# Spreading the roots' columns in a two-layer hybrid decoder trunk: transpositions on TensorE in place of fp32 products with the identity

## The chip, the core and the metric

The kernel runs on one core of a Trainium2 chip. Its time is the device time of one execution in microseconds (us); the median of several executions is given, with the lowest and the highest. Beside it stands one execution that was recorded by the hardware profiler: its span, its rows and its waits come from that execution alone.

## What is computed

The reference is a stack of two pre-norm residual layers over 1024 tokens of 1024 channels, in fp32, with a last RMSNorm. Each norm is followed by a shift and a scale from a conditioning vector. Cut to what matters here:

```python
def rms_norm(x, g):
    y = x * lax.rsqrt(jnp.mean(x * x, axis=-1, keepdims=True) + EPS)
    return y * g

for i in range(2):
    h = modulate(rms_norm(x, norm_mix_g[i]), sh_m, sc_m)
    y = conformer_conv(h) if i == 0 else multiscale_pool(h)   # the first has a LayerNorm inside
    x = x + (1.0 + g_m) * y
    h = modulate(rms_norm(x, norm_ffn_g[i]), sh_f, sc_f)
    x = x + (1.0 + g_f) * swiglu_ffn(h)
return rms_norm(x, final_g)
```

So each token has one reciprocal root per norm: two RMSNorms in each layer, the LayerNorm of the convolution module, and the last norm.

## The kernel before

Channels lie on the partitions and tokens along the free axis, in 8 tiles of 128 channels. The tokens are worked on in two chunks of 512, A and B, which are staggered: while one chunk is in its products, the other is in its norms. The large products are done in fp32r with three products for each tile of weights (high by high, high by low, low by high; `products`, line 496), so that TensorE has the longest queue. Part of the feed-forward products is done by a scheme with seven in place of eight products per block.

A norm needs a sum over channels, that is over partitions, for each token, and then the root of it along the free axis again, the same in every partition. `mean_rsqrt` (line 531) does it in these steps, and it is the one function that the change touches:

1. TensorE multiplies the squares, already summed over the 8 tiles, by a column of ones (lines 540 to 542). The sums of 512 tokens then stand as 4 columns of 128 partitions (the tile `var`).
2. VectorE works the reciprocal root out on those 128x4 values by eight or nine small instructions (`rsqrt`, line 504), into the tile `col`.
3. TensorE spreads each column along the free axis (line 558): the column, broadcast to 128x128, is the stationary operand and the identity the moving one, so that each of 128 output partitions receives the 128 roots in a row. The four results fill one PSUM bank (the tile `rstd`).
4. The norm multiplies the channels by it, from PSUM directly or from a copy by ScalarE (the tile `ny`).

`mean_rsqrt` is entered for twelve spreads: at the first norm of chunk A (line 1709), for that of chunk B, for the two LayerNorms (line 896), for the norms ahead of the feed-forward parts (lines 646 and 1284), for the pool layer's norms (line 956), for the last norm of A (line 1653), and for the two halves of the last norm of B (line 1577), which have two columns each; all others have four. The spread of column `i` is written as

```python
matmul(r[:, i * P : (i + 1) * P], col[:, i : i + 1].broadcast_to([P, P]), ident, start=True, stop=True)
```

The order of TensorE's instructions is the order in which the program emits them. That order is worked out while the program is built, by a planner with a clock for each engine: each product adds its price to `clock["PE"]` (line 147: 128 columns in fp32 cost `128 / 2400 * 4 + 0.0025` us), each instruction of VectorE and GpSimd adds a price to its own clock. After each unit of products, `pace` (line 224) emits waiting tasks of VectorE and GpSimd (norms, convolution taps, halves of weights) as long as the clock of their engine is less than 4 us ahead of TensorE's; `either` (line 179) gives an instruction to VectorE or GpSimd, whichever is free first by those clocks; and a task that has just asked for a root is not taken up again before `clock["PE"]` has moved on by the amount in `DELAY` (3.4 us for the spread, line 70). The instructions of the other engines are ordered by a scheduler from these.

Of the kernel before, what the change touches and what calls it, by code (L numbers as in the profile page):

```python
# [16 lines left out]
P = 128  # L17
# [114 lines left out]
def trunk(ctx, tc, xT, c, vec, ada, adan, w1f, w1, wdg, w2, wgu, wdn, wds, wpl, out):  # L132
    nc = tc.nc
    ctx.enter_context(tc.manual_schedule(engines={mybir.EngineType.PE}))
    clock = {"PE": 0.0, "V": 0.0, "G": 0.0, "S": 0.0}
# [5 lines left out]
    last_mm = [None]  # L141
# [3 lines left out]
    def matmul(out, lhsT, rhs, start, stop, more=False):  # L145
        n = out.shape[-1]
        clock["PE"] += n / 2400 * (1 if rhs.dtype == F32R else 4) + 0.0025
        last_mm[0] = nc.tensor.matmul(out, lhsT, rhs, start=start, stop=stop, skip_group_check=more).ins.name  # L148

    def order(ins):  # L150

        if behind[0] and last_mm[0] is not None:
            tc.add_manual_dep(ins.ins, last_mm[0], edge, reason="behind the products")
        return ins
# [41 lines left out]
    def nm(s):  # L196
        uid[0] += 1
        return f"{s}_{uid[0]}"
# [98 lines left out]
    def bank(name):  # L297
        return ps.tile([P, 512], F32, tag="mm", name=nm(name))

    def spare_bank(name):  # L300

        return ps.tile([P, 512], F32, tag="ca", name=nm(name), bufs=2)
# [11 lines left out]
    def temp(n, name="t", bufs=0):  # L314
        t = tmp.tile([P, TMPW], F32, tag=name if bufs else "t", name=nm(name), bufs=bufs or 4)
        return t[:, :n]
# [39 lines left out]
    ident = cst.tile([P, P], F32, name="ident")  # L356
# [80 lines left out]
    def ada_columns(js):  # L437


        todo = [(j, k) for j in js for k in range(KT)]  # L440
        src = lambda j, k: adan[k, :, (j - 2) * D : (j - 1) * D]
        ws = [ada_load(src(*t)) for t in todo[:ADA_BUFS]]
        for i, (j, k) in enumerate(todo):
            yield "load"
            if k == 0:
                acc = bank("ada")
            w = ws.pop(0)
            for g in range(4):
                matmul(acc[32 * g : 32 * g + 32, :Q], ccols[:, k, :], w[:, g * Q : g * Q + Q], start=k == 0, stop=k == KT - 1)
            clock["PE"] -= 1.3  # L450
            if i + ADA_BUFS < len(todo):
                ws.append(ada_load(src(*todo[i + ADA_BUFS])))
            if k == KT - 1 and (j != 3 or not held[0]):
                yield from columns_done(j, acc)
            elif k == KT - 1:
                held_back.append((j, acc))
# [3 lines left out]
    def columns_done(j, acc):  # L460

        rows = temp(Q)
        S_.copy(rows, acc[:, :Q])
        yield "spread"
        cols = bank("adac")
        for h in range(2):
            matmul(cols[:, 4 * h : 4 * h + 4], rows[:, h * P : h * P + P], quarters, start=True, stop=True)
        m = mod[:, j * KT : (j + 1) * KT]
        V_.tensor_tensor(m.rearrange("p (q h) -> p q h", h=2), cols[:, :KT].rearrange("p (h q) -> p q h", h=2),
                         V("ada_b", j * KT, KT).rearrange("p (q h) -> p q h", h=2), op=ADD)  # L470
        ada_gains(0, j, 0, KT, G_)
        ada_done.add((0, j))
# [23 lines left out]
    def products(out, wt, k, act, first, last, o=0, n=None, more=False):  # L496

        wk = slice(k * P, (k + 1) * P)
        for i, (wp, a) in enumerate(((0, 0), (0, 1), (1, 0))):
            cols = act[a][:, o : o + n] if n else act[a]  # L500
            matmul(out, wt[:, wp, wk], cols, start=first and i == 0, stop=last and i == 2, more=more)


    def rsqrt(v, y, t, q, alone):

        V_.tensor_scalar(y.bitcast(I32), v.bitcast(I32), -0.5, float(0x5F3759DF), op0=MUL, op1=ADD)
        yield
        V_.tensor_tensor(t, v, y, op=MUL)
        yield
        if not alone:  # L510
            V_.tensor_tensor(t, t, y, op=MUL)
            yield
            V_.tensor_scalar(q, t, 1.0, -10.0 / 3.0, op0=MUL, op1=ADD)
            yield
            V_.tensor_tensor(t, t, q, op=MUL)
            yield
        else:
            V_.tensor_tensor(q, t, y, op=MUL)
            yield
            V_.scalar_tensor_tensor(t, q, -10.0 / 3.0, q, op0=ADD, op1=MUL)  # L520
            yield
        V_.scalar_tensor_tensor(y, t, 5.0, y, op0=ADD, op1=MUL)
        yield
        V_.tensor_tensor(t, v, y, op=MUL)
        yield
        V_.scalar_tensor_tensor(t, t, -0.5 * 0.375**3, y, op0=MUL, op1=MUL)
        yield
        V_.scalar_tensor_tensor(y, t, 1.5 * 0.375, y, op0=ADD, op1=MUL)
        yield

    def mean_rsqrt(acc, n, keep=False, when="stats", loose=False, early=False):

        count = n // P
        parts = acc if isinstance(acc, list) else [acc]
        yield when
        b = bank("var")
        for i in range(count):  # L540
            for a in parts:
                matmul(b[:, i : i + 1], a[:, i * P : (i + 1) * P], ones[:, 0:1], start=a is parts[0], stop=a is parts[-1])
        v, t = b[:, :count], b[:, 16 : 16 + count]
        cols = tmp.tile([P, 16], F32, tag="col1", name=nm("col"), bufs=1)
        col, q = cols[:, :count], cols[:, 8 : 8 + count]
        for _ in rsqrt(v, col, t, q, "T" not in st or "taps_done" in st):
            if loose:
                yield
        V_.spent += 0.2
        clock["V"] += 0.2  # L550
        done = V_.last.ins.name
        for ins in [] if loose else recent + (beside if early else []) + [lows[id(wt)][0] for wt in st.get("loaded", [])[1:] if id(wt) in lows]:
            tc.add_manual_dep(ins, done, edge, reason="behind the root")
        recent.clear()
        yield "spread" if loose else "root"
        r = spare_bank("rstd") if "taps_done" in st else bank("rstd")
        for i in range(count):
            matmul(r[:, i * P : (i + 1) * P], col[:, i : i + 1].broadcast_to([P, P]), ident, start=True, stop=True)
        r = r[:, :n]
        if not keep:  # L560
            return r
        held = temp(n, "ny", 2)
        S_.copy(held, r)
        return held
# [54 lines left out]
    def rms(ch, keep=False):  # L619
        acc = yield from sum_sq(x[ch.i], ch.n)  # L620
        return (yield from mean_rsqrt(acc, ch.n, keep))
# [19 lines left out]
    def norm(ch, l, ffn, key, keep=False, squares=None):  # L641
        blocks = [block(f"h{ch.i}", "h") for _ in range(KT)]
        h = st[key] = [(b[:, 0], b[:, 1]) for b in blocks]
        st["blocks", ch.i] = blocks
        if squares is not None:
            rstd = yield from mean_rsqrt(squares.acc, ch.n, keep, loose=ch.i and not l)
        else:
            rstd = yield from rms(ch, keep)
        quiet[0] = ffn and not l
        for k in range(KT):  # L650
            if k == HOLD_TAPS:
                quiet[0] = False
            modulated(ch, l, ffn, h, rstd, k)
            yield
# [205 lines left out]
    def layer_norm_silu(ch):  # L860
# [30 lines left out]
        if ch.i == 0:  # L891
            for ins in beside:
                tc.add_manual_dep(ins, V_.last.ins.name, edge, reason="behind the sums")
            recent.extend(beside[2:])
            beside.clear()
        rstd = yield from mean_rsqrt(acc, n, when="settled" if ch.i else "stats", early=not ch.i)
        S_.activation(tmp.tile([P, 16], F32, tag="col0", name=nm("col"), bufs=1)[:, 0:1], acc[:, 0:1], AF.Silu)
        hv = [pair(f"h{ch.i}", "v") for _ in range(KT)]
# [1135 lines left out]
```

## Time and profile before

| | us |
|---|---|
| median of 3 executions | 1707.15 |
| lowest and highest | 1706.41 and 1709.43 |
| the profiled execution, its own time | 1708.65 |
| its span in the profile | 1706.9 |
| DVE busy | 1318.9 |
| ACT busy | 799.5 |
| POOL busy | 483.1 |

PE is TensorE's products, PEld its loads of stationary operands, DVE VectorE, ACT ScalarE, POOL GpSimd. "Busy" is the share of the span in which an engine ran an instruction; the products' ends are modelled, so a busy PE is not a PE at its peak. In the timeline's rows the columns are the start, the length, the engine, the line, the operation with output and inputs and shapes, and the count of instructions merged in the row; in brackets stands how long the engine was idle ahead of it, and what released it. In the chain's rows the columns are the start, the length, and the engine with the tile it wrote. The line is that of a helper in most rows (148 for products, 126 for the other engines), so that rows are told apart by their tiles.

The profiled execution took 1.75 us more than its span, which lies ahead of the first and behind the last recorded instruction, and 1.5 us more than the median of the three.

### The profile page before, as it was taken

The numbers are of one execution on the slowest core, as the hardware profiler recorded it, in microseconds if no ns is written. First come the engines' busy times: TensorE is split into PE (matmuls) and PEld (weight loads), VectorE is DVE, ScalarE is ACT, GpSimd is POOL, SyncE is SP. The second block draws the span as 40 slices with busy tenths as digits, with TensorE's granted clock in tenths as the row PEclk, the third lists the DMA queues.
The fourth block names the chain that finished last, engine by engine and source line by source line (L and its number), as shares of the span: only waits on it lengthen the run. The fifth ranks groups of instructions, "written<-read, shape, count | busy, mean of one in ns | idle before, by whom it ended". The sixth has DMA issues, their size and how long they took to land.

```text
span 1706.9 us, 21328 instructions
## 1 busy us (share of the span) xinstructions
PE 1671.0 (98%) x7614; PEld 1361.9 (80%) x7614; DVE 1318.9 (77%) x1872; ACT 799.5 (47%) x1085; POOL 483.1 (28%) x566
## 2 busy tenths in 40 slices
PE   7999999999999999999999999999999999999996
PEld 5777777778887888888888888888888888887776
DVE  8889899899659887878665987858777767657575
ACT  3669686866546333333213446637222222334353
POOL 3587767796001111211110311101111111010103
PEclk9999999999999999999999999999999999999998
DMA  8858987827776788986877757866777777486822
GB/s 303 286 168 228 237 229 196 220 96 225 225 238 152 253 272 279 294 249 229 342 256 264 250 173 206 241 237 190 189 209 234 217 229 217 169 294 191 241 93 99
DMA packets 115821, 380.71 MB, mean 223 GB/s; under 512 B 12225, under 2 KB 14401, under 8 KB 115714
## 3 DMA queue, kind: packets, MB, share of 16 engines
q1 hardware_dynamic: 77888, 247.46, 41.0%
q0 software_dynamic: 36736, 130.83, 31.2%
q8 instruction: 60, 0.98, 0.2%
q10 hardware_dynamic: 1090, 1.05, 0.2%
q14 instruction: 47, 0.39, 0.1%
HBM read 311.92 MB, written 63.18 MB: 220 GB/s over the span
## 4 chain that ended last, share of the span: by engine, by line
PE 86%; DVE 6%; DMA 3%; ACT 1%; issue 1%; POOL 1%; SPq 0%; DVEq 0%; ACTq 0%
PE a L148 23%; PE dn L148 21%; PE e L148 13%; PE p L148 12%; PE y L148 6%; PE g L148 3%; PE first L148 3%; PE tap L148 2%; DMA raw<-in_wds_dram 2%; POOL pa L126 1%; PE ada L148 1%; DVE t L126 1%; DMA adaw<-in_adan_dram 1%; DMA op<-kinds 1%; DVE x L126 1%
## 5 line engine op out<-in xcount | busy, mean ns | idle before, releaser
L126 ACT CAST w<-raw 128x1024 fp32r<-128x1024 f32 (+1 forms) x249 | 258.9, 1041 | 365.2 <-PE dn L148 99.7
L148 PE MATMUL dn<-g,w 128*128 128x512 f32 x1152 | 265.2, 391 | 1.7 <-DVE g L126 1.0
L126 DVE TENSOR_TENSOR w<-raw,w 128x1024 fp32r<-128x1024 f32 x177 | 217.7, 1233 | 51.2 <-ACT w L126 50.9
L148 PEld LDWEIGHTS dn<-g,w 128*128 128x128 f32 x1152 | 215.7, 188 | 47.6 <-DVE g L126 1.3
L148 PE MATMUL a<-n,w 128*128 128x512 f32 x1056 | 247.7, 390 | 1.1 <-DVE n L126 0.7
L148 PE MATMUL p<-h,w 128*128 128x512 f32 x1056 | 244.2, 391 | 0.9 <-DVE h L126 0.7
L126 POOL TENSOR_TENSOR pa<-pa,pr 128x512 f32<-128x512 f32 x160 | 228.4, 1512 | 23.0 <-ACT pr L126 16.6
L148 PEld LDWEIGHTS a<-n,w 128*128 128x128 f32 x1056 | 197.9, 188 | 44.0 <-DVE n L126 2.2
L148 PEld LDWEIGHTS p<-h,w 128*128 128x128 f32 x1056 | 197.3, 188 | 43.8 <-DVE h L126 1.5
L148 PE MATMUL dn<-hi,w 128*128 128x512 f32 (+1 forms) x600 | 174.3, 373 | 4.3 <-DVE x L126 2.4
L126 DVE SCALAR_TENSOR_TENSOR ca<-u,vecs,ca 128x512 f32<-128x512 f32 x245 | 169.7, 745 | 0.5
L126 DVE SCALAR_TENSOR_TENSOR x<-dn,gains,x 128x512 f32<-128x512 f32 (+1 forms) x144 | 100.9, 730 | 44.7 <-PE dn L148 44.6
L148 PEld LDWEIGHTS dn<-hi,w 128*128 128x128 f32 x600 | 109.8, 188 | 25.6 <-DVE x L126 3.2
L148 PE MATMUL a<-t,w 128*128 128x512 f32 x528 | 123.6, 390 | 0.7 <-DVE w L126 0.7
L148 PE MATMUL e<-b,w 128*128 128x512 f32 x528 | 123.4, 390 | 0.6 <-DVE r L126 0.6
L148 PE MATMUL e<-t,w 128*128 128x512 f32 x528 | 123.3, 389 | 0.0
L126 ACT ACTIVATE pr<-u,vecs 128x512 f32<-128x512 f32 x160 | 108.2, 716 | 26.0 <-POOL pa L126 18.2
L148 PEld LDWEIGHTS a<-t,w 128*128 128x128 f32 x528 | 99.0, 188 | 21.6 <-DVE w L126 1.1
L148 PEld LDWEIGHTS e<-b,w 128*128 128x128 f32 x528 | 99.1, 188 | 21.5 <-DVE r L126 1.0
L1108 POOL DMA_DIRECT2D raw<-in_wgu_dram x41 | 36.2, 884 | 282.5 <-DVE r L126 78.3
L148 PEld LDWEIGHTS e<-t,w 128*128 128x128 f32 x528 | 99.1, 188 | 20.5
L148 PE MATMUL dn<-lo,w 128*128 128x512 f32 (+1 forms) x300 | 111.7, 372 | 0.0
(181 smaller groups left out, 2380.2 us busy)
## 6 DMA issues: line engine op xcount, KB each, us to landing
raw<-in_wgu_dram SPq DMA_DIRECT2D x132, 512.0 KB, 4.8
adaw<-in_ada_dram POOLq DMA_DIRECT2D x48, 512.0 KB, 7.3
raw<-in_wdn_dram SPq DMA_DIRECT2D x44, 512.0 KB, 8.1
raw<-in_wgu_dram POOLq DMA_DIRECT2D x41, 512.0 KB, 7.4
raw<-in_w_dram SPq DMA_DIRECT2D x36, 512.0 KB, 6.2
gd<-g POOLq DMA_DIRECT2D x36, 512.0 KB, 8.1
g<-gd SPq DMA_DIRECT2D x36, 512.0 KB, 6.0
kinds<-k POOLq DMA_DIRECT2D x33, 512.0 KB, 7.3
```

What stands on the lines that cost most here:

```text
L126: self.last = self.order(getattr(self.eng, name)(out, *args, **kw))
L148: last_mm[0] = nc.tensor.matmul(out, lhsT, rhs, start=start, stop=stop, skip_group_check=more).ins.name
L1108: d = order(nc.gpsimd.dma_start(w[i], wgu[l, fp, src], accum_op=ADD))
```

## The change

The spread calls a new helper, which issues a transposition on TensorE with the same two operands (the broadcast column and the identity) into the same place, and adds another price to the planner's clock: `128 / 2400 + 0.0025` us for each column in place of `128 / 2400 * 4 + 0.0025`.

```diff
+    def turned(out, columns):
+
+        clock["PE"] += P / 2400 + 0.0025
+        last_mm[0] = nc.tensor.transpose(out, columns, ident).ins.name
...
         r = spare_bank("rstd") if "taps_done" in st else bank("rstd")
         for i in range(count):
-            matmul(r[:, i * P : (i + 1) * P], col[:, i : i + 1].broadcast_to([P, P]), ident, start=True, stop=True)
+            turned(r[:, i * P : (i + 1) * P], col[:, i : i + 1].broadcast_to([P, P]))
         r = r[:, :n]
```

Number and shape of the tiles, the transfers, the waits and the work of the other engines are as before.

## The prediction

> **What bounds the kernel now.** I read the page first, for the engine that has no air, then the rows of the one tile that the change touches, then the chain of waits at each of its twelve places.
>
> ```profile
> span 1706.9 us, 21328 instructions
> PE 1671.0 (98%) x7614; PEld 1361.9 (80%) x7614; DVE 1318.9 (77%) x1872; ACT 799.5 (47%) x1085; POOL 483.1 (28%) x566
> PE 86%; DVE 6%; DMA 3%; ACT 1%; issue 1%; POOL 1%; SPq 0%; DVEq 0%; ACTq 0%
> ```
>
> TensorE is busy in 98% of the span and holds 86% of the chain (third row). So time taken out of its queue counts, unless what follows there waits for another engine anyway.
>
> ```profile
> L148 PEld LDWEIGHTS rstd<-ident,col x96: 184/190/338, 15.7 to 1698.9; 128*128 128x128 f32 x96
> L148 PE MATMUL rstd<-ident,col x96: 270/275/578, 15.7 to 1699.1; 128*128 128x128 f32 x96
> ```
>
> These are all the spreads (lowest, median and highest duration of one record, in ns). The code calls eleven spreads of four columns and two halves of two, which share one of the twelve places: 48 products, but 96 records, so an fp32 product is two loads and two multiplications. The 275 ns of a record isn't its cost, since records overlap; the cost is read from starts:
>
> ```profile
> 1170.28 1.05 PE L148 MATMUL rstd<-ident,col 128*128 128x128 f32 x8
> 1171.09 2.09 PE L148 MATMUL p<-h,w 128*128 128x512 f32 x8
> ```
>
> The eight records hold the queue from 1170.28 to the next product's start at 1171.09: 0.81 us, 0.101 us a record. The sums, in the same view:
>
> ```profile
> 941.67 0.95 PE L148 MATMUL var<-ones,acc 128*128 128x1 f32 x8
> 942.48 4.33 PE L148 MATMUL dn<-g,w 128*128 128x512 f32 x18
> ```
>
> The sums `var` also have eight records and stationary tiles of 128x128, but a moving side of one column in place of 128, and take the same 0.81 us (941.67 to 942.48). So what sets the pitch is the load of the stationary tile, and not the columns that stream.
>
> **The change part by part.**
>
> *Removed: half of the records, I estimate.* A transposition isn't in this trace. The nearest row for a product of one pass is an fp32r one:
>
> ```profile
> L148 PE MATMUL y<-v,w 128*128 128x512 f32 x384 | 89.2, 392 | 0.5 <-DVE v L126 0.5
> ```
>
> The code calls 2 chunks x 8 outputs x 8 inputs x 3 = 384 of these: one record each. A transposition only moves values, and needs no pass for the low half of an operand, so I take one record per column: four in place of eight. At the pitch of 0.101 us for a stationary 128x128 tile this is 0.40 us in place of 0.81, a gain of **0.405 us at each place of four columns**. From below: the shortest pitch of the trace is that of `ada` (next fence: eight records from 227.60 to 228.17, 0.071 us each, with a load of 32 columns), which would give 0.28 us and a gain of 0.53. From above: a transposition that can't overlap its load or its neighbour costs a load and a record from the two `rstd` rows, 0.190 + 0.275 = 0.465 us, 1.86 us in all, a loss of 1.05. I take 0.101, since the `var` and `rstd` rows have the same load, and keep both ends.
>
> The Trainium skill's page "TensorE: Matmul & The Clock Gate" (Terms) calls the transpose mode 4x faster for FP32. By that a place would take 0.81 / 4 = 0.20 us, and the sum below would be an estimated -5.8 us; the `var` rows, where the load binds, speak against it, and no run here shows it.
>
> *Places where the gain reaches the end.* In the chain of waits the spread itself stands at these places:
>
> ```profile
> 102.64 0.89 PE rstd L148 x8
> ...
> 300.43 0.91 PE rstd L148 x8
> ...
> 511.15 0.91 PE rstd L148 x8
> ...
> 1029.43 0.89 PE rstd L148 x8
> ...
> 1170.44 0.89 PE rstd L148 x8
> ```
>
> From 300 to 511 there are three, with one at 442 between them; VectorE's next step in the chain starts from them. From 1029 to 1170 there are three, with one at 1068; products stand before and behind them. Six places x 0.405 = **-2.43 us**.
>
> At 102 it also stands between products, but what it gains meets the next place:
>
> ```profile
> 227.60 0.64 PE L148 MATMUL ada<-adaw,ccols 128*32 128x256 f32 x8
> 228.17 1.16 PE L148 MATMUL rstd<-ident,col 128*128 128x128 f32 x8
> ...
> 229.37 3.08 DVE L126 TENSOR_TENSOR u<-u,rstd 128x512 f32<-128x512 f32 x5 [0.16 <-PE rstd L148]
> ```
>
> VectorE waited only 0.16 us for this spread, and the chain then runs along VectorE until 247. What 102 and 228 gain together, 0.81 us, arrives only as 0.16, unless VectorE has less in front of it. Between 0.16 and 0.81 I take the middle, **-0.5 us**.
>
> ```profile
> 945.31 2.37 DVE adaw L126 x4
> ...
> 960.90 1.20 PE dn L148 x4
> ```
>
> At 946 (spread from 946.65) the chain goes past the spread on VectorE, and the products at 960.90 come behind it. Between 0 and 0.405 I take **-0.2 us**.
>
> *Places where it doesn't.* At the start:
>
> ```profile
> 15.72 2.05 PE L148 MATMUL rstd<-ident,col 128*128 128x128 f32 x8 [2.12 <-DVE col L126]
> ```
>
> ```profile
> 16.63 1.22 DVE L126 TENSOR_TENSOR w<-raw,w 128x1024 fp32r<-128x1024 f32 x1
> 17.77 0.20 DVE L126 TENSOR_SCALAR mod<-mod,vecs 128x1 f32<-128x1 f32 x1
> 17.89 0.74 DVE L126 SCALAR_TENSOR_TENSOR t<-x,gains,rstd 128x512 f32<-128x512 f32 x1
> ```
>
> ```profile
> 19.40:60.90 41.50, 41.47 (x170) 32.61 (x170) 41.50 (x60) 13.99 (x17) 20.52 (x6) 1.00 0.75 273
> ```
>
> The spread (first row) would end about 1 us earlier, but VectorE works on `w` and `mod` until it takes `t` up at 17.89 with no wait (next rows). And then it is busy without a gap: the last row is a window with its length and the busy time of PE, PEld, DVE, ACT and POOL, and VectorE has 41.50 of 41.50 us. I take **0**; if the scheduler puts `t` ahead of `w`, up to -1.0. The cover is VectorE's order alone. At 1685.9:
>
> ```profile
> 1686.60 0.42 ACT t L126
> 1687.02 0.55 ACT ny L126
> ```
>
> ScalarE reads that spread at 1687.02, right behind `t`, and the chain goes on along VectorE: **0**.
>
> *The tail.* The two spreads of two columns stand on the chain:
>
> ```profile
> 1692.70 0.93 PEld L148 LDWEIGHTS rstd<-ident,col 128*128 128x128 f32 x4 [3.82 <-DVE col L126]
> 1693.51 0.55 PEld L148 LDWEIGHTS var<-ones,acc 128*128 128x128 f32 x2
> ```
>
> ```profile
> 1692.60:1693.60 1.00, 0.90 (x4) 0.90 (x4) 0.00 (x0) 0.00 (x0) 0.50 0.90 342
> ```
>
> ```profile
> 1692.70 1.23 PE rstd L148 x4
> ...
> 1698.30 1.21 PE rstd L148 x4
> ```
>
> After an idle stretch the granted clock is 0.50 (the window's row, behind the busy times) and the pitch (1693.51 - 1692.70) / 4 = 0.20 us. Two records less are 0.41 us, twice: **-0.8 us**, at most half of 1.23 and 1.21, that is -1.2, each spread being released by `col` and followed at once in the chain.
>
> *The planner.* Each spread adds 4 x (128 / 2400 x 4 + 0.0025) = 0.863 us to its clock of TensorE before, and 0.223 us after; measured are 0.81, and expected 0.40. So the planner sees TensorE 0.64 us earlier behind each spread, emits about that much less of VectorE's and GpSimd's work ahead, and may place it, or a later spread, behind another unit of products. No work is added. No row prices this; I take **0**, and bound it by the rival below. There is no new wait, transfer or tile; no instruction moves past a DMA queue by the edit itself.
>
> **Sum:** -2.43 - 0.5 - 0.2 - 0.8 = **-3.9 us**. The profiled execution took 1708.65 us (span 1706.9 and 1.75 around it), so it would take 1704.7; it stood 1.5 above the median of 1707.15, and the same sum from the median gives **1703.2 us**. By the lower ends of the terms (-2.43, -0.16, 0, -0.8) the sum is -3.4, by the upper ends at the same pitch (0.81, 0.405, 1.0 and 1.2 in their places) -5.8.
>
> **The rivals.**
>
> *The planner gives it back.* For: VectorE is busy 77% of the span, all of the time at the start, so that a low half of a weight or a norm that is emitted one unit later can be late. What such a lateness costs is shown by one row of PE's waits (total, times, longest):
>
> ```profile
> PE dn L148 <- DVE x L126: 2.6, 3, 1.6
> ```
>
> Two new waits of 1.6 us are 3.2 and leave 1706.4; more than four of them, 7.3 us in all, would be needed for a loss of 3.4. Against: waits of this kind sum to little in 1707 us, and a shift may as well take one away (then about 1700).
>
> *Nothing is overlapped (slower).* If a transposition's load can't run beside the multiplication before it, at each place TensorE takes 0.465 us a column: +1.05 at six places is +6.3, +1.6 at the three half-covered ones (half of 3 x 1.05), and at the tail two columns at 0.338 + 0.578 (the highest durations in the two `rstd` rows) take 1.83 in place of 0.82, +2.0 for both: +9.9 us, **1717 us**. It decides from a pitch of 0.81 / 4 = 0.203 us on; twice that of the same load now. For it speaks only that no such instruction is in the trace.
>
> *A record costs its whole duration.* With 0.275 us a column (the median of the `rstd` row) a place takes 1.10 us, +0.29, and at nine places, three of them at half, +2.2; the tail gains 0.82 - 0.55 = 0.27 twice. Together +1.7 us, **1708.8**. The Trainium skill's page "TensorE: Matmul & The Clock Gate" (Part 4: PE-mode transpose) gives about 275 ns per 128x128 bf16 transposition within a kernel, with the full clock not engaged; the fp32 product's record here has that very duration and yet a pitch of 0.101 us, so I read the page's figure as a duration. No run here shows a transposition yet.
>
> *It does nothing.* If a transposition in fp32 still leaves two records a column, the time is 1707.2, moved by the planner alone.
>
> **How the numbers follow.** A measurement of this kernel can tell about 0.2% from no change, which is 3.4 us: 1703.7 to 1710.6 is "the same", so that my forecast lies just beyond the bound. Forecast (-3.4 to -5.9): 0.48. The planner gives it back in part (to within 0.2%): 0.28. The planner adds to it (below -5.9): 0.06. The planner costs more than the gain (over +3.4): 0.06. Whole durations, or no effect: 0.06 together, the same. Nothing overlapped: 0.06, slower. So faster 0.48 + 0.06 = 0.54, same 0.28 + 0.06 = 0.34, slower 0.06 + 0.06 = 0.12. The range goes from 1699 (the pitch of `ada`, or a wait less) to 1709 (whole durations); left out are about two in ten, the slow cases and half of the fastest.
>
> **What the profile would show.** `rstd` has 48 records in place of 96, and the next product starts 0.40 us behind the spread's first record (over 0.81: a rival). At the tail the two chain pieces fall from 1.2 to 0.8 us. `t` at the start still begins about 17.9. If PE's busy time falls by about 4 us and the span doesn't, the planner's shifts ate it, and rows of PE's waits have grown. The prediction is wrong if records are still 96, if the pitch is above 0.2 us, or if a wait of more than 2 us stands where none was.

## The result, and the profile after

The changed kernel took 1719.34 us (median of 4, 1718.12 to 1719.61), the kernel before 1708.29 us beside it (median of 4): a ratio of 1.0063, with a 95% interval of 1.0046 to 1.0081. A second set of executions on another occasion (below) gave 1.0077 (1.0064 to 1.0090). So the change made the kernel 11 to 14 us slower, where 3.9 us were forecast in its favour.

The head of the page of the changed kernel:

```profile
span 1716.3 us, 21217 instructions
PE 1667.2 (97%) x7566; PEld 1355.4 (79%) x7566; DVE 1324.9 (77%) x1872; ACT 799.0 (47%) x1085; POOL 483.5 (28%) x566
```

TensorE has 48 records less (7566) and is busy for 3.8 us less (1667.2 in place of 1671.0). That this is almost the forecast's 3.9 is partly chance: stretches at half the clock, of which more at the end, lengthen the busy time of the changed kernel. And the span is 9.4 us longer: TensorE is idle for 13 us more. The view of the tile `rstd`, and rows of TensorE's timeline at two spreads:

```profile
L153 PEld LDWEIGHTS rstd<-ident,col x48: 133/136/230, 16.0 to 1706.6; 128*128 128x128 f32 x48
L153 PE MATMUL rstd<-ident,col x48: 270/272/444, 16.0 to 1706.8; 128*128 128x128 f32 x48
```

```profile
229.83 0.65 PE L153 MATMUL rstd<-ident,col 128*128 128x128 f32 x4
230.24 2.09 PE L148 MATMUL a<-h,w 128*128 128x512 f32 x8
...
1184.25 0.60 PE L153 MATMUL rstd<-ident,col 128*128 128x128 f32 x4
1184.60 1.64 PE L148 MATMUL p<-h,w 128*128 128x512 f32 x6
```

One record per column, and four of them hold the queue for 0.41 and 0.35 us, 0.09 to 0.10 us each, in place of 0.81. The instruction does what was forecast of it.

Where the time went is seen in windows of 40 us (start and end, length, busy time of PE with its records, granted clock, DMA share and GB/s). First the kernel before, then the changed one:

```profile
360.00:400.00 40.00, 38.58 (x169) 1.00 0.56 152
400.00:440.00 40.00, 40.00 (x181) 1.00 0.51 177
440.00:480.00 40.00, 39.80 (x180) 1.00 0.85 263
```

```profile
360.00:400.00 40.00, 35.96 (x153) 0.96 0.48 131
400.00:440.00 40.00, 38.39 (x168) 1.00 0.50 161
440.00:480.00 40.00, 34.09 (x148) 0.91 0.81 240
```

In these 120 us TensorE was idle for 1.42 + 0 + 0.20 = 1.6 us before and for 4.04 + 1.61 + 5.91 = 11.6 us after. What it waited for is in the list of PE's waits of the changed kernel (total, times, longest); its two first rows, for `col` (7.5 us) and `acc` (6.1), are left out, since they stand in the kernel before too (7.8 and 5.7):

```profile
PE y L148 <- ACT v L126: 4.3, 1, 4.3
PE dn L148 <- DVE g L126: 4.0, 1, 4.0
PE dn L148 <- DVE x L126: 3.7, 4, 1.6
PE first L148 <- ACT h L126: 3.0, 1, 3.0
...
PE y L148 <- DVE v L126: 1.9, 2, 1.6
PE first L148 <- DVE h L126: 1.5, 2, 1.3
```

The row for `g` of the kernel before is this one, and it has none of products `y`:

```profile
PE dn L148 <- DVE g L126: 1.0, 1, 1.0
```

Three places stand out. *The LayerNorm of chunk B*: the products `y` of the convolution module's end wait for its results `v`. On TensorE that LayerNorm has three small groups, `mean`, `var` and `rstd`, among long runs of other products. Before:

```profile
422.58 1.02 PE L148 MATMUL mean<-acc,ones 128*128 128x512 f32 x2
...
437.06 0.95 PE L148 MATMUL var<-ones,acc 128*128 128x1 f32 x8
...
442.04 1.05 PE L148 MATMUL rstd<-ident,col 128*128 128x128 f32 x8
...
455.69 19.66 PE L148 MATMUL y<-v,w 128*128 128x512 f32 x86
```

And after:

```profile
433.50 1.02 PE L148 MATMUL mean<-acc,ones 128*128 128x512 f32 x2
...
455.33 0.95 PE L148 MATMUL var<-ones,acc 128*128 128x1 f32 x8
...
461.67 0.60 PE L153 MATMUL rstd<-ident,col 128*128 128x128 f32 x4
466.53 0.79 PE L148 MATMUL y<-v,w 128*128 128x512 f32 x1 [4.26 <-ACT v L126]
468.97 6.41 PE L148 MATMUL y<-v,w 128*128 128x512 f32 x20 [1.65 <-DVE v L126]
```

From the spread to the first `y` there were 13.65 us before, filled with other products, while VectorE and ScalarE made `v`. Now the spread comes 19.6 us later and nothing is left to fill in. The order of TensorE's instructions, taken as a list without the tiles' buffer numbers, differs in nothing else: these three groups alone have moved, the mean by 8 groups of three products, the var by 16 and the spread by 18, which is 18 x 3 = 54 products of about 0.227 us or 12 us.

*Near 366 us* products of the feed-forward part wait 4.0 us for VectorE's `g`, in place of 1.0. *At the start* VectorE has another order (so the waits are not as before, as the section on the change has it):

```profile
18.06 0.75 DVE L126 SCALAR_TENSOR_TENSOR t<-x,gains,rstd 128x512 f32<-128x512 f32 x1
18.72 0.21 DVE L126 TENSOR_SCALAR mod<-mod,vecs 128x1 f32<-128x1 f32 x1
20.05 0.75 DVE L126 SCALAR_TENSOR_TENSOR h<-t,mod,h 128x512 fp32r<-128x512 f32 x1 [1.12 <-ACT h L126]
```

`t` now stands ahead of `mod`, and ScalarE's `h`, which needs both, comes later: the first product starts 4.1 us behind the spread's start (20.07 from 16.01), in place of 3.7 (19.41 from 15.72), and the waits that follow make it more. From the start of the first sums `var` to the first product `a` behind that stage it took 66.22 - 11.74 = 54.5 us before and 68.44 - 12.12 = 56.3 us after.

### The profile page after: what moved, and what is told of

The parts are those of the page before. It is cut to its first block, busy times and chain, and to the rows that moved or that the text cites. A ratio compares the mean times of both kernels' runs of the same rounds, so it can differ in the third digit from the quotient of the medians.

```text
span 1716.3 us, 21217 instructions
## 1 busy us (share of the span) xinstructions
PE 1667.2 (97%) x7566; PEld 1355.4 (79%) x7566; DVE 1324.9 (77%) x1872; ACT 799.0 (47%) x1085; POOL 483.5 (28%) x566
## 4 chain that ended last, share of the span: by engine, by line
PE 81%; issue 7%; DVE 6%; DMA 2%; POOL 2%; ACT 1%; POOLq 0%; SPq 0%; DVEq 0%; ACTq 0%
PE a L148 23%; PE dn L148 19%; PE e L148 13%; PE p L148 12%; PE y L148 6%; PE g L148 3%; PE first L148 2%; PE tap L148 2%; DVE ca L126 1%; PE ada L148 1%; DVE u L126 1%; DMA adaw<-in_adan_dram 1%; DVE t L126 1%; POOL x L126 1%; DVE w L126 1%
```

## The experiments

Theory 1: the transposition gains what was forecast, and the loss comes from the planner, whose clock the change lowered. Its rival: the transposition itself costs, by something around it that the rows don't show. Ratios are to the kernel before, executed beside each set on the same chip (1707.65, 1707.20 and 1707.15 us), with 95% intervals; they come from all executions, and so are not always the quotient of the medians beside them. The edits are cut to the lines that matter, and shown against the version that the text names.

### Price and instruction apart

The first run keeps the transposition and the old price, the second the product and the new price. Both edits are of the changed kernel.

```diff
     def turned(out, columns):
-        clock["PE"] += P / 2400 + 0.0025
+        clock["PE"] += P / 2400 * 4 + 0.0025
         last_mm[0] = nc.tensor.transpose(out, columns, ident).ins.name
```

> Transpositions as in the changed kernel, but the planner's clock is charged the old 0.2158 us per column, so TensorE's instructions stand in the order of before. Theory 1 (the time was lost to the planner's order, and the transposition itself gains): the late second LayerNorm spread (461.7 us) goes back to about 442 us, TensorE is busy again for at least 38 of each 40 us between 360 and 480; the start still loses some 2 us, since VectorE's order there is not the planner's; the places gain 3.4 to 3.9 us: 1706 to 1707.5 us against 1708.3 before, ratio 0.999. Rival (the transposition itself costs, say by a switch of mode around it): above 1715 us, as in the changed kernel.

Measured: 1706.6 us, 0.9990 (0.9979 to 1.0001). The spread of that LayerNorm stands at 443.19 us again, and the first stage takes 68.55 - 12.09 = 56.5 us, as in the changed kernel.

```diff
     def turned(out, columns):
         clock["PE"] += P / 2400 + 0.0025
-        last_mm[0] = nc.tensor.transpose(out, columns, ident).ins.name
+        last_mm[0] = nc.tensor.matmul(out, columns, ident, start=True, stop=True, skip_group_check=False).ins.name
```

> The fp32 products of before, but the planner's clock is charged the new 0.0558 us per column: TensorE's order is that of the changed kernel. Theory 1: the loss is there without any transposition, and 3.4 to 3.9 us more than it for the spreads, less some 2 us at the start, where VectorE's order should be that of before: 1719 to 1722 us, ratio 1.0065 to 1.008, with TensorE idle some 10 us between 360 and 480 us. Rival: 1708 us as before.

Measured: 1723.97 us, 1.0094 (1.0078 to 1.0111), a little more than expected. There is no transposition in this kernel, and it is the slowest of all. Its windows are those of the changed kernel:

```profile
360.00:400.00 40.00, 35.94 (x152) 0.96 0.55 151
400.00:440.00 40.00, 38.39 (x168) 1.00 0.48 152
440.00:480.00 40.00, 32.35 (x142) 0.91 0.84 249
```

So the rival falls: with the products of before, one line of the program that computes nothing on the chip costs 16 us by itself.

### The start

The old price is kept in both runs. In the first the first norm's spread stays a product; in the second all are transpositions, and one dependency puts `t` behind `mod`.

```diff
-    rstd_p = now(mean_rsqrt(acc, A.n))
+    rstd_p = now(mean_rsqrt(acc, A.n, product=True))
```

> Old price, transpositions at all places but the first, which keeps its fp32 products. Theory 2 (the transposition at the first place makes the scheduler put VectorE's t ahead of mod, which costs some 2 us by 68 us): the first product starts again 1.65 us behind the spread, the 192 first products take 47 us in one stretch, and the time is 1704.0 to 1705.0 us, ratio 0.9975 to 0.998, about 2 us under the run with all transpositions at the old price. Rival (the start's loss comes from the transfers there and differs from run to run): the same as that run within 1 us.

```diff
             V_.tensor_scalar(mod[:, k : k + 1], mod[:, k : k + 1], V("ada_b", k), None, op0=ADD)
+            mod_first = V_.last.ins.name
...
             t_last = V_.last.ins.name
+            if k == 0:
+                tc.add_manual_dep(V_.last.ins, mod_first, edge, reason="the shift first")
```

> Old price, transpositions at all twelve places, and one dependency added at the first norm: VectorE's t stands behind its mod, as in the kernel of before. Theory 2: the start of before is back with the transposition in it, so the time is that of the run with products at the first place, 1704.0 to 1705.0 us (ratio 0.9975 to 0.998); the first place gains 0 by the prediction. Rival: the order of t and mod doesn't matter, and the run stays at 1706 to 1707.5 us, like the one with all transpositions at the old price.

Measured: 1703.78 us, 0.9983 (0.9971 to 0.9995), and 1705.23 us, 0.9984 (0.9974 to 0.9993), both just beside what was expected. In both the 192 first products run in one stretch again:

```profile
19.86 46.99 PE L148 MATMUL first<-h,w 128*128 128x512 f32 x192 [2.61 <-ACT h L126]
```

(this row is of the run with the dependency), and the first stage takes 54.2 us (66.31 - 12.07 and 66.69 - 12.46). In all ten traces of this document in which `mod` stands ahead of `t`, that stage takes 54.2 to 54.6 us, and in the three others 56.3 to 56.5. So the order of `t` and `mod` costs 2 us in the trace. The times alone would not have shown it: their intervals overlap with those of the first run. The two runs agree with each other, so the transposition at the first place gains nothing once `mod` stands first, as forecast. The planner's price has no part in this: with the transposition and the old price `t` stands ahead, with the product and the new price behind. The order at the start is that of the scheduler; that it takes `t` up sooner because the spread ends earlier there fits, but was not shown.

### The late LayerNorm alone

Back to the run with the old price and the dependency, and one delay of the planner raised (`settled_b` has the value of the old `settled`), so that `mean`, `var` and `rstd` of that LayerNorm stand exactly where the changed kernel has them and all other instructions of TensorE stand as before. The list of GpSimd stays the same too, and those of VectorE and ScalarE change between 430 and 480 us alone. A second run goes half as far.

```diff
-DELAY = {..., "root": 3.4}
+DELAY = {..., "root": 3.4, "soon_b": 6, "settled_b": 3}
...
-        yield "soon" if ch.i else "stats"
+        yield "soon_b" if ch.i else "stats"
```

> The run with all transpositions, the old price and the shift first, with one delay raised (the second LayerNorm's sum from 0.5 to 6 us), so that the three small groups of that LayerNorm on TensorE (mean, var, rstd) stand exactly where they stand in the changed kernel, and every other TensorE instruction where it stood. Theory 3 (the late place of that LayerNorm carries the loss): TensorE idles 6 to 10 us more between 430 and 480, and the time is 1711 to 1715 us, ratio 1.002 to 1.005 against before. Rival (the loss comes from VectorE's order of taps and halves of weights, which the price changed too, above all the wait of 4 us near 366): at most 1707 us.

> As the run before, with the delay at 4 us: the mean stands half as far behind (4 groups of three products, 2.7 us), the var 8 and the rstd 10 groups (5.4 and 6.8 us). Theory 3: between, 1706 to 1711 us, since the products of the y follow 6 us nearer to the spread than before but VectorE has some air. Rival: as the run without the delay, 1705 us.

Measured: 1715.24 us, 1.0054 (1.0041 to 1.0066), and with the delay at 4 us 1709.02 us, 1.0011 (1.0002 to 1.0019). Against 0.9984 without the delay that is 0.70%, 12 us, and 0.27%, 4.6 us: more than the upper end of what I had expected for the first. The waits are the changed kernel's:

```profile
PE dn L148 <- DVE x L126: 5.4, 5, 1.9
PE y L148 <- ACT v L126: 4.1, 1, 4.1
...
PE y L148 <- DVE v L126: 2.3, 2, 2.1
```

while the wait for `g` near 366 us is 1.0, as before. TensorE's idle time between 400 and 480 is 7.8 us (1.61 + 6.20) against 0.7 without the delay. Of the other 4 to 5 us, some 2.5 are the clock: it stands at 0.50 from 460.7 to 467.5 us (more on this at the end), and TensorE is busy for 5 us of that. Another 2 us arise between 1200 and 1680 us (busy 476.15 against 478.25), where the order is the same and single traces differ by as much.

### How much of the discount does it take?

The price is lowered at all spreads but the second (chunk B's first norm); and then to 0.101 us a column at all of them, the pitch that was measured. Both keep the dependency at the start, and both leave TensorE's order as before. The edits are shown against the run with the old price and the dependency.

```diff
-        clock["PE"] += P / 2400 * 4 + 0.0025
+        clock["PE"] += P / 2400 * (4 if spreads[0] == 1 else 1) + 0.0025
```

> Transpositions and shift first, the new low price at all spreads but the second (chunk B's first norm, at 102 us), which is charged the old one: three quarters of the discount stay, yet TensorE's order is that of before. Theory 4 (a threshold: only the discount of the three spreads ahead of the second LayerNorm together moves it behind a further unit): 1703.5 to 1706.5 us, ratio 0.997 to 0.999. Rival (the low price hurts in proportion, through VectorE's order): 1709 to 1716 us.

```diff
-        clock["PE"] += P / 2400 * 4 + 0.0025
+        clock["PE"] += 0.101
```

> Transpositions and shift first, each charged 0.101 us, the pitch that the changed kernel's trace shows. TensorE's order is that of before. Theory 4: 1703.5 to 1706.5 us, ratio 0.997 to 0.999, like the old price. Rival (any lower price costs): 1709 us or more.

Measured: 1710.09 us, 1.0016 (1.0008 to 1.0025), and 1703.63 us, 0.9981 (0.9973 to 0.9990). The first missed its expectation: although TensorE's order is that of before, 0.32%, 5.5 us, are lost against the old price. One wait shows the most of it (PE's wait near 366 us; first this run, then the one with the measured price):

```profile
PE dn L148 <- DVE g L126: 3.8, 1, 3.8
```

```profile
PE dn L148 <- DVE g L126: 1.2, 1, 1.2
```

The wait is 2.6 us longer, and behind it the granted clock is 0.50 from 364.7 to 368.1 us with TensorE busy, which costs 1.7 more; the two profiled spans differ by 3.9 us (1705.1 and 1701.2). The profiled execution is the fastest of this run; what makes the median 3.3 us longer no trace shows.

So the price acts in two ways. The start ends with a line that sets the planner's clocks equal, so that the first spread's discount is lost there; three spreads lie between it and that LayerNorm. With the discount of 0.64 us at two of them, VectorE's list is changed so that `g` comes 2.6 to 3 us too late; with all three, the LayerNorm also moves behind further products. With 0.46 us at all three (0.863 - 4 x 0.101) neither happens. So `g` doesn't go by the sum of the discounts: 1.28 us in two steps made it late, 1.38 in three did not. "Only the order on TensorE counts" was too narrow a theory; what stands is that the planner's list counts, on two engines. The rows show what changed ahead of `g`: in the five traces where it is late, VectorE runs five convolution taps between that `g` and the one before it, and takes 7.7 us from the end of one to the end of the other; in the eight others it runs three or four and takes 6.6. That is 1.1 us; where the rest of the lateness arises was not singled out.

### Do the parts add up?

The changed kernel with only the dependency at the start; the changed kernel itself; and the version with the measured price, all on one chip.

> The changed kernel (transpositions, low price) with only the dependency added that puts VectorE's t behind its mod at the first norm. TensorE's order is that of the changed kernel. If the start is a cost of its own, beside the late LayerNorm and the wait near 366 us: 2.1 us under the changed kernel on the same chip, ratio 1.005 to 1.008 against before. Rival (what the start loses is caught up by the waits behind it, which go by VectorE and GpSimd): the same as the changed kernel within 0.7 us.

> The changed kernel once more, beside the others on one chip and with more executions. If the parts found so far add up (places -2.7, late LayerNorm +12, wait near 366 us +4, start +2): ratio 1.007 to 1.009. If they overlap: 1.0046 to 1.0065.

> The version with transpositions, 0.101 us a column and the shift first, again on this chip: 0.997 to 0.999 against before, and below the changed kernel by 0.8 to 1.1%.

Measured: 1717.14 us, 1.0059 (1.0046 to 1.0071); 1720.70 us, 1.0077 (1.0064 to 1.0090); 1703.73 us, 0.9979 (0.9970 to 0.9988). The start is worth 0.18% (3.1 us, with intervals that just overlap, against 2 in the traces), so it is not caught up by later waits. The parts are the late LayerNorm +12, the wait near 366 us +5.5, the start +2 and the transpositions -2.7 to -3.6: some +16 to +17 us, where the changed kernel has 13 (11 to 15). (The expectation, 1.007 to 1.009, held; it reckoned with +4 for the wait.) Without the start it is +14 to +15 from the parts and +10 (8 to 12) measured. So the parts overlap by some 3 to 5 us. A reason would be that a product that waits for VectorE near 366 leaves VectorE more time for what comes next; no run shows it.

The version with the measured price and the dependency beats both kernels: 3.2 and 3.6 us under the kernel before, 17.0 us under the changed one beside it (1703.73 and 1720.70).

## Why the prediction was wrong

**Right: the instruction.** One record per column, 0.09 to 0.10 us each, at a full granted clock. The "nothing overlapped" rival, whose 1717 us come near the measured time, is out: its pitch of 0.465 us is nowhere in the trace, and with the old price and `mod` first the transpositions make the kernel faster. That its number came near is chance. The figure of about 275 ns in the Trainium skill's page "TensorE: Matmul & The Clock Gate" (Part 4) is, as forecast, a duration: a transposition's record lasts 272 ns here, while four of them hold the queue for 0.35 to 0.41 us. The factor of 4 for FP32 in the Trainium skill's same page (Terms) did not show: four columns fell from 0.81 to 0.35 to 0.41 us, a factor of 2.0 to 2.3.

**Nearly right: the sum of the places.** -3.9 us was forecast; with TensorE's order kept and the start mended, 0.9984, 0.9981 and 0.9979 were measured, -2.7 to -3.6. By its terms: the tail gained 1.1 us, a little more than the 0.8 forecast (each piece of the chain 1.2 before, now 0.69 and 0.67 us in the version with the measured price):

```profile
1687.63 0.69 PE rstd L153 x2
...
1692.56 0.67 PE rstd L153 x2
```

The three late places gained what was forecast: from the sums `var` at 1024 us to the product behind the spread at 1170 it takes 146.80 us before and 145.57 in the version with the old price and the dependency, 1.23 us less (three times 0.405 is 1.22). The early places gained less. From the first `a` at 66 us to those sums the terms promise 1.9 us (0.5, three times 0.405 and 0.2); five traces with transpositions, TensorE's old order and an early `g` gained 1.3, 1.1, 0.6, 0.35 and 0.1, the last with a granted clock of 0.50 for 3.4 us near 93 us. I had carried the gains at 300, 442 and 511 through without asking what stood behind them. At 442 the products behind the LayerNorm start when ScalarE's `r` is there, at the same time in the kernel before (first) and in the version with the old price and the dependency (second):

```profile
450.12 5.73 PE L148 MATMUL p<-h,w 128*128 128x512 f32 x24 [0.20 <-ACT r L126]
```

```profile
450.11 5.73 PE L148 MATMUL p<-h,w 128*128 128x512 f32 x24 [0.66 <-ACT r L126]
```

At 300 VectorE's first `h` behind the spread starts 0.41 us earlier in that version, but takes 1.63 in place of 1.18 us and ends at 304.2 in both, and the products `p` start at 308.23 in place of 308.19, with a wait of 0.79 in place of 0.34. So what TensorE gains there ends in a wait.

**Wrong, and it decided: the planner.** "No row prices this; I take 0" and the rival's price of "two new waits of 1.6 us" were the step that failed; in its place the runs showed three groups moved by up to 12 us (+12 us by themselves) and a late `g` (+5.5). The prediction's own sign of being wrong, a wait of more than 2 us where none was, came true at `y` (4.3 us), and the wait for `g` grew from 1.0 to 4.0. I took the price of a lateness from the waits that the old order had, which are the short ones exactly because that order was good; a moved group is priced by how far it moves. A unit of products is 24 x 0.227 = 5.4 us, and the spread moved by 12 us. The row that would have bounded it was in the trace: from the spread at 442.04 to `y` at 455.69 there were 13.65 us, in which VectorE and ScalarE, with other work between, made `v` (VectorE's last piece ended at 458.4, behind the start of `y`); a delay of 12 us could not be free there. The discount was also taken spread by spread (0.64 us), where three of them add up (1.9 us) ahead of the one place that has no slack. A chance of 0.06 for this loss was far too low, and the range ended below it.

**Wrong in sign: the start.** I bounded it by 0 and -1.0 us, by `t` moving ahead of `w`. It moved ahead of `mod`, which its reader ScalarE needs too, and cost 2 us. An earlier input was taken for a gain or nothing, but it also changes what the scheduler takes next.

## What to carry to other kernels

Where a program works out its order from a model of times, an edit of an instruction's price is an edit of the whole order: time it by itself, with the old instruction, before the sum of the instruction's own gain is believed. Compare the lists of instructions of both kernels first; three groups that moved by up to 12 us were the bulk of this result, and no duration of any instruction showed them. Charge a new instruction with its measured pitch: with all else equal, a price that is too low by nearly half (0.056 in place of 0.101 us) cost 13 us here (1717.14 against 1703.73), against a gain of 3. A price twice too high, the old one, did as well as the measured one (0.9984 and 0.9981).

## What the runs showed of the hardware

The waits of TensorE were dearer than their length. In the changed kernel, windows of 2 us behind the spread of the late LayerNorm (busy time and records of PE, then the granted clock):

```profile
462.00:464.00 2.00, 0.27 (x3) 1.00 1.01 412
464.00:466.00 2.00, 0.00 (x0) 0.89 0.83 338
466.00:468.00 2.00, 0.79 (x1) 0.50 0.44 131
468.00:470.00 2.00, 1.03 (x3) 0.50 0.68 201
470.00:472.00 2.00, 2.00 (x6) 0.50 0.92 346
472.00:474.00 2.00, 2.00 (x9) 0.90 1.06 227
474.00:476.00 2.00, 2.00 (x11) 1.00 0.98 225
```

The last record of the spread ends at 462.27. With 1.00 ahead of it and 0.50 behind, the mean of 0.89 in the second window means that the clock fell at about 465.6, after 3.3 us without a product, and the 0.90 in the sixth that it rose again at about 472.4; for 4.2 us of that time TensorE was busy at half speed (6 products in 2 us, where 11 are run later). So the waits of 4.3 and 1.65 us cost some 2 us more. Near 366 us, behind the wait of 4.0 us, windows of 1 us show the same: 0.79 from 366 to 367, then 0.50 up to 370, then 1.00. The Trainium skill's page "TensorE: Matmul & The Clock Gate" (Part 1) puts a window of about 3.4 us on the fall and on the return of the clock. The slow stretches agree with it: from 465.6 to 472.4 it is 6.8 us, twice 3.4, and from 366.6 to 370.0 it is 3.4. The distance to the products is less fixed. The clock fell 3.3 us behind the last product here and 3.8 near 366; it rose 3.4 us behind the start of steady products here (468.97) and 3.2 there, but 5.1 in the run with the delay at 6 us (462.41 to 467.5).

And between 1200 and 1680 us, where TensorE's order is the same in all versions, it was idle for 1.7 us in some traces and 4.4 in others (busy 478.27 with the measured price, 475.56 before, 475.77 with the first product kept), so that single traces of this kernel can't be compared to better than 2 to 3 us.
